# Projection tiles of the prologue as matmul pairs over two column halves of the array

## The chip, the cores and the metric

The kernel runs on one core of one Trainium2 chip. The metric is device time in microseconds (us), lower is better. Per core there are TensorE (PE in the profile; its weight loads are listed as PEld), VectorE (DVE), ScalarE (ACT), GpSimd (POOL) and SyncE (SP), which issues nearly all DMAs here. A matmul holds one operand in the array (128 rows by 128 columns, the "weights", brought in by a weight load of its own) and streams the other one past it; its result goes to PSUM, whose 128 partitions correspond to the columns of the array.

## The reference

One encoder layer over 1024 tokens of width 1024, float32 (cut to what matters):

```python
h = jnp.einsum('bsd,de->bse', x, w_in[layer])
q_a, k_a, v_a, z_a, q_b, k_b, v_b, z_b = jnp.split(h, SPLIT_POINTS, axis=-1)
y_a = neighborhood_attention(q_a, k_a, v_a, rel_pos_bias[layer])      # 8 heads of 64
qb, kb = rotary(q_b, positions), rotary(k_b, positions)
y_b = windowed_gqa_with_sink(qb, kb, v_b, sink_logits[layer])         # 8 q heads, 2 kv heads
mixed = jnp.concatenate([y_a * jax.nn.silu(z_a), y_b * jax.nn.silu(z_b)], axis=-1)
y = jnp.einsum('bse,ed->bsd', mixed, w_out[layer])
x = layer_norm(DEEPNORM_ALPHA * x + y, ln_gain[layer], ln_bias[layer])
```

The projection `x @ w_in` without the v columns is 21 tiles of 128 output columns: four each of q, k and z for group A, four each of qb and zb and one kb for group B.

## The kernel before, in words

Float32 accuracy is had from float16 pairs: x and the weights are scaled by powers of two and split into a high and a low part (`x16h`, `x16l`; `h`, `l` of a weight tile), and a product is three matmuls, high x high, high x low and low x high, summed in PSUM.

The kernel has these stages. The first 59 us bring in x, project v (line L486: tokens as weights, 320 columns of v streamed), and find the scales. Then `project(name)` computes one tile of 128 output columns at a time: for each of two halves of the 1024 tokens it takes a PSUM bank (tag "pj", two of them in turn) and runs 8 blocks of 128 along the width, three products each, so 24 matmuls of 128 x 128 weights with 512 streamed columns into one accumulation group; then `evac` hands the bank to ScalarE, VectorE and GpSimd, which turn it into what q, k or z need. `ORDER` lists the tiles; the first `NPRO = 6` of them (zb0, z0, zb1, kb, qb0, z1) run back to back as a prologue between 59 and 122 us. The other 15 are cut into single matmuls and filled in between the steps of the attention (`pump_to`), which runs from 122 to some 350 us: scores (L816, L817), softmax, products with v (L881). The output projection (L1031) and the layer norm end the kernel.

The order of the instructions of each engine is written by hand: `project` is a generator that yields behind each matmul, `run_to(c)` pumps the prologue matmul by matmul, and `events` are called at fixed counts of yielded steps. In the prologue these events and `project` itself put other work on TensorE between the projection's matmuls: `w_scale` (L225), which sums a statistic of a weight tile over all partitions by one matmul of 2 columns (15 the last time), five times; and `v_scale` (L672), one float32 transpose. These use the whole array. `w_split` readies the weight tiles two ahead (high part on ScalarE, L199, low part on GpSimd, L204 and L205), `sum_w` (L702) and `v_part` (L685, L693) are further work of the prologue on ScalarE and VectorE.

Of the kernel before, what the change touches and what calls it, by code (L numbers as in the profile page):

```python
# [20 lines left out]
KT = D // 128  # L21
# [10 lines left out]
NPRO = 6  # L32
# [29 lines left out]
def hybrid_block(ctx, tc, xT, x, wt, wv, wo, bias, sink, gain, lbias, cos, sin, bmask, out):  # L62
    nc = tc.nc
# [10 lines left out]
    def bank(tag):  # L74
        bufs = {"pj": 2, "s": 4, "t": 2}[tag]
        return (ps1 if bufs == 1 else ps2).tile([128, 512], F32, tag=tag, name=f"ps_{tag}", bufs=bufs)
# [98 lines left out]
    def need(*ops):  # L175
        for op in ops:
            if op.step is None:
                need(*op.deps)
                queues[op.eng].remove(op)
                op.emit()  # L180
# [10 lines left out]
    def w_split(m):  # L191
        if m >= NH:
            return

        def hi():
            h = wp.tile([128, 4, 128], F16, tag="wh", name=f"wh{m}", bufs=4)
            l = wp.tile([128, 4, 128], F16, tag="wl", name=f"wl{m}", bufs=4)
            parts[m] = (h, l)
            nc.scalar.activation(h, raws[m], AF.Copy, scale=scale)  # L199

        def lo():
            h, l = parts[m]
            raw = raws.pop(m)
            nc.gpsimd.tensor_scalar(raw, raw, scale, 1.0, op0=ALU.mult, op1=ALU.mult)  # L204
            nc.gpsimd.tensor_sub(l, raw, h)  # L205

        g = min(m // 2, NPRO)
        scale = wsc[:, g:g + 1]

        o = enq("act", hi, load_ops.get(("w", m)), prio=0.5)  # L210
        o = enq("pool", lo, o, prio=0.5)
        w_ops[m] = o
        if m + 5 < NL:
            load_ops["w", m + 5] = enq("sp", lambda: w_load(m + 5), o)
# [3 lines left out]
    def w_scan(m):  # L218
        nc.scalar.activation(junk[:, :512], raws[m].rearrange("p k c -> p (k c)"), AF.Abs, accum_out=wm[:, m:m + 1])

    def w_scale(n):
        g, v = wg[:, n:n + 1], inv[:, n:n + 1]
        c, m = (2 * n, 2) if n < NPRO else (2 * NPRO, NS)
        ps = bank("t")
        nc.tensor.matmul(ps[:, :m], ones, wm.bitcast(BF16)[:, 2 * c + 1:2 * (c + m):2], start=True, stop=True)  # L225
        nc.vector.tensor_reduce(g, ps[:, :m], axis=mybir.AxisListType.X, op=ALU.add if n < NPRO else ALU.max)
        nc.vector.tensor_scalar_max(g, g, 2.0 ** -30)
        nc.vector.tensor_scalar(g.bitcast(I32), g.bitcast(I32), 0x7F800000, None, op0=ALU.bitwise_and)
        nc.vector.tensor_scalar(wsc[:, n:n + 1].bitcast(I32), g.bitcast(I32), 0x7F800000, None, op0=ALU.bitwise_xor)
        nc.vector.tensor_scalar(v, g, xrs, 0.5, op0=ALU.mult, op1=ALU.mult)  # L230
        nk, nq = ORDER.index("kb"), ORDER.index("qb0")
        if n >= NPRO - 1:
            i = n - NPRO + 1
            nc.vector.tensor_scalar_mul(invt[:, i:i + 1], v, 0.5)
        if n == NPRO:
            for i, (a, b) in enumerate(((nk, nq), (nk, NPRO), (NPRO, NPRO))):
                nc.vector.tensor_scalar(sg[:, i:i + 1], inv[:, a:a + 1], inv[:, b:b + 1], -0.125 / QSCALE ** 2,
                                        op0=ALU.mult, op1=ALU.mult)
            nc.vector.reciprocal(rsg, sg[:, 2:3])
            nc.vector.tensor_reduce(zi[:, 0:1], inv, axis=mybir.AxisListType.X, op=ALU.max)  # L240
            nc.vector.reciprocal(zi[:, 1:2], zi[:, 0:1])
            nc.vector.tensor_scalar_mul(zc[:, 0:1], zi[:, 1:2], MSCALE)
            for i, a in ((1, NPRO - 1), (2, NPRO)):
                nc.vector.tensor_scalar(zc[:, i:i + 1], inv[:, a:a + 1], zi[:, 1:2], 0.5 * MSCALE, op0=ALU.mult, op1=ALU.mult)
            nc.vector.tensor_scalar(mc, zi[:, 0:1], vsc, 0.5 / MSCALE, op0=ALU.mult, op1=ALU.mult)
# [72 lines left out]
    def evac(name, half, ps):  # L318
        sl = slice(512 * half, 512 * half + 512)
        kind = name.rstrip("0123")  # L320
        p = int(name[-1]) if name[-1].isdigit() else 0
        n = ORDER.index(name)
        if kind in ("kb", "qb"):
            raw, o1, o5 = rope(ps, half)
            if kind == "kb":
                split_k("b", half, raw, o5)
            else:
                split_q(f"b{p}", half, raw, o5)
            return [o1]
        if kind == "k":  # L330
            return split_k(p, half, ps)
        if kind == "q":
            return split_q(p, half, ps)
        e = 4 + p if kind == "zb" else p
        if half == 0:
            zt[e] = zslot(f"z{e}", ZTAG.get(name, "z"))
        if name in ORDER[:3]:
            nc.scalar.activation(zt[e][:, sl], ps, AF.Silu, scale=inv[:, n:n + 1])
            return []
        half_inv = invt[:, 0:1] if n < NPRO else invt[:, 1:2]  # L340
        o = enq("act", lambda: nc.scalar.activation(zt[e][:, sl], ps, AF.Tanh, scale=half_inv), prio=0)
        o2 = enq("dve", lambda: nc.vector.scalar_tensor_tensor(
            zt[e][:, sl], zt[e][:, sl], 1.0, ps, op0=ALU.add, op1=ALU.mult), o, prio=0)
        stk_ops.setdefault(name, []).append(o2)
        return [o2]
# [7 lines left out]
    def new_group():  # L353
        if len(groups) >= 2:
            need(*groups[-2])
        return bank("pj")

    def project(name):
        n = ORDER.index(name)
        w_split(2 * n + 2)  # L360
        for half in range(2):
            ps = new_group()
            for k in range(KT):
                if k % 4 == 0:
                    need(w_ops[2 * n + k // 4])
                h, l = parts[2 * n + k // 4]
                if n + 2 < NPRO and half == 0 and k == 4:
                    w_scan(2 * n + 4)
                if n + 2 < NPRO and half == 1 and k == 0:
                    w_scan(2 * n + 5)  # L370
                if half == 0 and k == 4:
                    w_split(2 * n + 3)
                if n + 2 < NPRO and half == 1 and k == 6:
                    w_scale(n + 2)
                for i, (a, b) in enumerate(((h, x16h), (h, x16l), (l, x16h))):
                    mv = b[half, k]
                    if name[0] == "q" and name[1] != "b":
                        mv = mv.rearrange("p (r b c) -> p b r c", b=4, r=8)
                    nc.tensor.matmul(ps, a[:, k % 4, :], mv,  # L379
                                     start=(k == 0 and i == 0), stop=(k == KT - 1 and i == 2))  # L380
                    if not (k == KT - 1 and i == 2):
                        yield
            groups.append(evac(name, half, ps))
            yield
# [20 lines left out]
    with ExitStack() as vctx:  # L405
# [4 lines left out]
        ps = bank("t")  # L410
# [235 lines left out]
        for a in range(2):  # L646
            ps = bank(tags[4 + a])
# [67 lines left out]
        for i in range(NS):  # L715
            at(14 + 14 * i, sum_w, i)
        at(219, w_scale, NPRO)
        fill.extend(project(n) for n in ORDER[:NPRO])
        run_to(100)

# [191 lines left out]
    for b in range(4):  # L912
        at(WIN_AT[b], window, b)
    run_to(48 * NPRO)
    fill.extend(project(n) for n in FILL)
    FILL_N = [48] * len(FILL) + [9, 9, 6, 12, 24]
    pumped = [0]
# [407 lines left out]
```

## Time and profile before

| | us |
|---|---|
| median of 3 runs | 445.9 (445.83 to 446.32) |
| profiled execution, span from its first to its last instruction | 444.7 |
| TensorE busy | 437.5 (98%) |
| VectorE busy | 344.2 (77%) |
| ScalarE busy | 308.3 (69%) |
| GpSimd busy | 221.6 (50%) |

The page gives the profiled execution's own time as its span; the median of the runs stands 1.2 us above it. Busy time of TensorE counts a matmul from its start to its modelled end, and successive matmuls overlap, so a busy share does not tell how fast they follow one another; that is read from the starts in the timeline, or from the chain, which gives the length of a piece and its number of matmuls. "PEclk" is the granted clock of TensorE in tenths of full speed.

### The profile page before, as it was taken

How to read it: one execution, taken by the hardware profiler on the slowest of the kernel's cores; microseconds unless marked ns; L12 is line 12 of the kernel's file. 1: busy time of each engine (PE TensorE's matmuls, PEld its weight loads, DVE VectorE, ACT ScalarE, POOL GpSimd, SP SyncE). 2: the span in 40 equal slices, each digit the busy share in tenths (PEclk: the TensorE clock that was granted, in tenths of full speed). 3: DMA queues.
4: the chain of work that ended last, by engine and by line, in shares of the span. 5: the costliest groups of instructions: out<-in, count | busy, mean ns of one | idle time of the engine just before them, and what ended most of it. 6: DMA issues, size and time to landing. Idle time of an engine off the chain costs nothing.

```text
span 444.7 us, 9505 instructions
## 1 busy us (share of the span) xinstructions
PE 437.5 (98%) x3289; PEld 255.5 (57%) x3289; DVE 344.2 (77%) x849; ACT 308.3 (69%) x700; POOL 221.6 (50%) x235
## 2 busy tenths in 40 slices
PE   9999999999999999999999999999999999999994
PEld 8997754444445565655565655656555654444453
DVE  5978967438986898887988888888878837589944
ACT  5759789766499988887868887888778946302401
POOL 0110074646839558866506767765574405205740
PEclk9999999999999999999999999999999999999997
DMA  8921469984659999587978899998999998103612
GB/s 272 390 91 60 145 235 339 336 292 169 213 127 214 206 190 181 98 162 143 164 127 175 169 182 180 213 170 213 192 204 253 167 172 347 55 0 102 232 69 72
DMA packets 133841, 81.39 MB, mean 183 GB/s; under 512 B 101280, under 2 KB 113440, under 8 KB 133536
## 3 DMA queue, kind: packets, MB, share of 16 engines
q1 hardware_dynamic: 133648, 80.64, 75.4%
q8 instruction: 26, 0.43, 0.4%
q14 instruction: 23, 0.19, 0.2%
q10 hardware_dynamic: 144, 0.13, 0.1%
HBM read 50.34 MB, written 9.96 MB: 136 GB/s over the span
## 4 chain that ended last, share of the span: by engine, by line
PE 91%; DMA 3%; POOL 3%; DVE 1%; issue 1%; ACT 1%; SPq 0%; POOLq 0%; DVEq 0%; ACTq 0%
PE ps_pj L379 44%; PE ps_s L1031 9%; PE ps_s L486 6%; PE ps_t L881 6%; PE ps_pj L1031 5%; PE ps_t L1031 5%; PE ps_s L816 4%; PE ps_s L817 4%; PE ps_pj L486 3%; PE ps_t L486 3%; DMA bias<-in_bias 3%; PE ps_t L901 1%; POOL wl L205 1%; PE ps_t L412 1%; POOL ks L295 1%
## 5 line engine op out<-in xcount | busy, mean ns | idle before, releaser
L379 PE MATMUL ps_pj<-xf,wh 128*128 128x512 f16 x672 | 202.1, 379 | 0.1
L379 PE MATMUL ps_pj<-xf,wl 128*128 128x512 f16 x336 | 127.3, 379 | 0.0
L379 PEld LDWEIGHTS <-wh 128*128 128x128 f16 x672 | 63.7, 98 | 60.4 <-DVE ks L263 0.5
L842 ACT ACTIVATE ps_s<-sn,nm 128x385 f32<-128x385 f32 (+3 forms) x128 | 70.1, 548 | 25.1 <-DVE nm L826 24.6
L853 DVE SCALAR_TENSOR_TENSOR split<-ps_s,split 128x384 f16<-128x384 f32 (+2 forms) x128 | 65.7, 513 | 27.5 <-ACT split L852 25.9
L1031 PEld LDWEIGHTS <-m 128*128 128x128 f16 x432 | 40.0, 98 | 41.1 <-DVE m L939 0.2
L852 ACT ACTIVATE split<-ps_s 128x384 f16<-128x384 f32 (+2 forms) x128 | 57.8, 452 | 2.5 <-DMA tr<-split 0.2
L204 POOL TENSOR_SCALAR wr<-wr,wsc 128x512 f32<-128x512 f32 x26 | 20.6, 791 | 68.1 <-ACT wh L199 61.6
L379 PEld LDWEIGHTS <-wl 128*128 128x128 f16 x336 | 32.9, 98 | 37.4
L826 DVE CUSTOM_DVE_ANT_0 sn<-ps_s,bm,nsk 128x384 f32<-128x384 f32 (+1 forms) x64 | 40.7, 636 | 2.0 <-PE ps_s L817 1.7
L1031 PE MATMUL ps_s<-wo,m 128*128 128x512 f16 (+1 forms) x192 | 40.8, 366 | 0.0
L816 PE MATMUL ps_s<-ks,qs 128*128 128x384 f16 (+4 forms) x128 | 39.2, 306 | 0.3 <-DVE qs L263 0.3
L817 PE MATMUL ps_s<-ks,qs 128*128 128x384 f16 (+4 forms) x128 | 39.2, 306 | 0.0
L826 DVE CUSTOM_DVE_ANT_0 sn<-ps_s,bias,sg 128x264 f32<-128x264 f32 (+1 forms) x64 | 35.0, 547 | 4.5 <-issue 1.5
L881 PEld LDWEIGHTS <-tr 128*128 128x128 f16 (+1 forms) x1104 | 36.6, 98 | 2.2
L205 POOL TENSOR_TENSOR wl<-wr,wh 128x512 f16<-128x512 f32 x26 | 32.7, 1257 | 2.2
L788 POOL TENSOR_SCALAR bias<-bias,rsg 128x552 f32<-128x552 f32 (+1 forms) x24 | 19.1, 797 | 23.8 <-DMA bias<-in_bias 22.6
L295 POOL COPY ks<-ks 64x512 f16<-64x512 f16 x40 | 26.0, 661 | 7.1 <-DVE ks L263 2.8
L1086 ACT ACTIVATE sd<-mv,eps 128x1 f32<-128x1 f32 x8 | 2.4, 295 | 36.5 <-DVE mv L1084 35.2
L1031 PE MATMUL ps_pj<-wo,m 128*128 128x512 f16 (+1 forms) x144 | 26.2, 326 | 0.0
L1130 POOL TENSOR_TENSOR xr<-xr,gb 128x512 f32<-128x512 f32 x7 | 9.8, 1396 | 32.4 <-ACT xr L1127 32.4
L842 ACT ACTIVATION_READ_ACCUMULATOR ps_s<-sn,nm 128x1 f32 x128 | 24.4, 190 | 0.0
(188 smaller groups left out, 813.8 us busy)
## 6 DMA issues: line engine op xcount, KB each, us to landing
ws<-in_wt SPq DMA_DIRECT2D x15, 512.0 KB, 5.9
wr<-in_wt SPq DMA_DIRECT2D x26, 256.0 KB, 3.6
wor<-in_wo SPq DMA_DIRECT2D x22, 256.0 KB, 3.5
bias<-in_bias SPq DMA_DIRECT2D x16, 276.0 KB, 3.3
xr<-in_x SPq DMA_DIRECT2D x8, 512.0 KB, 9.6
out<-xr SPq DMA_DIRECT2D x15, 256.0 KB, 2.1
bias<-in_bias SPq DMA_DIRECT2D x8, 368.0 KB, 3.8
wvraw<-in_wv SPq DMA_DIRECT2D x9, 320.0 KB, 5.8
```

Source lines behind the costliest of these rows:

```text
L205: nc.gpsimd.tensor_sub(l, raw, h)
L295: nc.gpsimd.tensor_copy(t[o, sl], t[a, sl])
L379: nc.tensor.matmul(ps, a[:, k % 4, :], mv, start=(k == 0 and i == 0), stop=(k == KT - 1 and i == 2))
L486: nc.tensor.matmul(ps[:, :320], lh[:, ts], rh[:, cs], start=(k == ko[0] and i == 0), stop=(k == ko[-1] and i == 2))
L816: nc.tensor.matmul(ps[:, :m], q, sl[0], start=True, stop=False)
L817: nc.tensor.matmul(ps[:, :m], q, sl[1], start=False, stop=True)
L826: nc.vector.tensor_tensor_reduce(sn[:, :m], ps[:, :m], bias_t, sg[:, c:c + 1], init, op0=ALU.add, op1=ALU.min, accum_out=nm)
L842: nc.scalar.activation(pt[:, :m], sn[:, :m], AF.Exp, bias=nm, scale=-1.0, accum_out=sm[:, k:k + 1])
L852: nc.scalar.activation(hl[:, :m, 0, :c], src, AF.Copy, scale=PSCALE)
L853: nc.vector.scalar_tensor_tensor(hl[:, :m, 1, :c], src, PSCALE, hl[:, :m, 0, :c], op0=ALU.mult, op1=ALU.subtract)
L881: nc.tensor.matmul(ps[:, HD * m:HD * m + HD], a, b_, start=(i == 0), stop=(i == len(mms) - 1))
L1031: nc.tensor.matmul(ps, lh[:, ts], rh[:, cs], start=(e == EO[0] and i == 0), stop=(e == EO[-1] and i == 2))
```

## The change

For a tile of the prologue (`n < NPRO`), each of the 288 matmuls over the whole array becomes two: one with the weight columns 0 to 63 into PSUM partitions 0 to 63, one with the weight columns 64 to 127 into partitions 64 to 127. Both stream the same 512 columns of x, and each has a weight load of 64 columns ahead of it. In the program's instructions they occupy a tile of 128 rows by 64 columns of the array, the second at column 64. The tiles filled into the attention stay as they are.

```diff
                     mv = b[half, k]
                     if name[0] == "q" and name[1] != "b":
                         mv = mv.rearrange("p (r b c) -> p b r c", b=4, r=8)
-                    nc.tensor.matmul(ps, a[:, k % 4, :], mv,
-                                     start=(k == 0 and i == 0), stop=(k == KT - 1 and i == 2))
+                    for c in (slice(0, 64), slice(64, 128)) if n < NPRO else (slice(0, 128),):
+                        nc.tensor.matmul(ps[c], a[:, k % 4, c], mv,
+                                         start=(k == 0 and i == 0), stop=(k == KT - 1 and i == 2))
                     if not (k == KT - 1 and i == 2):
                         yield
```

The `yield` stays where it was, behind the pair, so the counts at which events are called are unchanged. The order of the instructions on VectorE, ScalarE, GpSimd and SyncE is the same as before, and on TensorE the pairs stand where the single matmuls stood. The first matmul of the second to fifth tile has a wait on an earlier matmul of TensorE's own.

## The prediction

> **What bounds the kernel now.** I read the page's busy times first, then the chain of waits that ended last in order of time, then the busy times of the stretch in which the prologue's projections run, then the waits of TensorE, and last TensorE's groups by shape and its timeline.
>
> The busy times and the throttle row of the 40 slices say which engine to look at:
>
> ```profile
> span 444.7 us, 9505 instructions
> PE 437.5 (98%) x3289; PEld 255.5 (57%) x3289; DVE 344.2 (77%) x849; ACT 308.3 (69%) x700; POOL 221.6 (50%) x235
> PEclk9999999999999999999999999999999999999997
> PE 91%; DMA 3%; POOL 3%; DVE 1%; issue 1%; ACT 1%; SPq 0%; POOLq 0%; DVEq 0%; ACTq 0%
> ```
>
> TensorE is busy for 98% of the span at nearly full clock and makes up 91% of the chain. A busy TensorE can still be one that is badly fed, so the stretch itself must be read. The chain, in order of time, gives it in pieces (start, length, what):
>
> ```profile
> 53.02 6.52 PE ps_t L486 x48
> 59.54 3.45 PE ps_pj L379 x16
> 62.99 0.11 PE ps_s L672
> 63.10 5.61 PE ps_pj L379 x26
> 68.71 0.00 PE ps_t L225
> 68.72 10.38 PE ps_pj L379 x48
> ...
> 107.02 14.91 PE ps_pj L379 x69
> 121.93 0.11 PE ps_s L816
> ```
>
> The six tiles are the L379 matmuls from 59.5 to 121.9 us: 6 tiles x 2 token halves x 8 k blocks x 3 products = 288. One piece holds 48 of them in 10.38 us, so one costs 216.25 ns of TensorE, and 288 cost 62.3 us. The chain hands them on from one to the next with no wait between; the little matmuls of L225 in between take 0.00 of it and the one of L672 takes 0.11. The stretch as a whole, and the waits of TensorE over the whole kernel:
>
> ```profile
> 59.37:121.77 62.40, 62.40 (x297) 28.44 (x294) 41.21 (x93) 45.25 (x81) 38.40 (x39) 1.00 0.79 259
> PE ps_t L1111 <- ACT dr L1109: 1.8, 1, 1.8
> PE ps_t L412 <- DVE warm L127: 1.0, 1, 1.0
> PE ps_s L816 <- DVE qs L263: 0.3, 1, 0.3
> ```
>
> In the stretch's row the columns are length, then busy time of PE, its weight loads, VectorE, ScalarE and GpSimd, the granted clock (1.00), the DMA share and GB/s. TensorE fills all 62.40 us; the next engine, ScalarE, fills 45.25. In the whole kernel TensorE waits 3.1 us for others, and none of that lies between 59 and 122 us. So what the edit does to the spacing of these matmuls goes to the end of the span one for one: no engine waits ahead of them that could give time back, and what follows is again TensorE's own queue.
>
> **The change, part by part.** Each of the 288 matmuls of 128 array columns becomes two of 64, each with a weight load of its own; both stream the same 512 columns of x. TensorE issues 288 matmuls and 288 weight loads more; no other engine's instruction, order or DMA changes. The accumulation groups of the halves lie on different partitions of the same bank, and the evacuation waits for the second half's last matmul.
>
> *The streams.* First, what a matmul costs. The L486 piece has 48 matmuls of 320 columns in 6.52 us, 135.8 ns each; 216.25 less 135.8 over 192 columns is 0.419 ns a column, so 512 columns take 214.5 ns and the fixed part is 1.7 ns. The time is that of the streamed columns. Half the array's columns make a stream no shorter. If the halves stream one after the other, a pair costs 432.5 ns; if they stream side by side, 216 ns. The trace has no matmul on part of the columns, so the two ends are +62.3 us and, if the fixed part were hidden too, 288 x 1.7 = -0.5 us. I take side by side, +0: the halves share no array column, no PSUM partition and no wait, so nothing in the program orders them. The nearest rows show TensorE holding two matmuls in flight: a record lasts 379 ns where the spacing is 216.
>
> ```profile
> L379 PE MATMUL ps_pj<-xf,wh 128*128 128x512 f16 x672 | 202.1, 379 | 0.1
> L379 PEld LDWEIGHTS <-wh 128*128 128x128 f16 x672 | 63.7, 98 | 60.4 <-DVE ks L263 0.5
> 149.73 1.13 PE L881 MATMUL ps_t<-vb,tr 128*128 128x64 f16 x33
> ```
>
> The Trainium skill, page "TensorEngine Tiling (Array Packing)", section "Key Properties", says that different tiles can execute weight loads and matmuls in parallel; no row here shows it.
>
> *Issue and weight loads.* The L881 row has 33 matmuls of 64 columns, each with its own load of 128 columns, in 1.13 us less the last one's drain of 0.16 (379 - 216 ns): some 29 ns for load and matmul together. So TensorE issues two such couples within 60 ns, well under 216. Each load must lie beside the stream of the other half. That loads lie beside streams is what the timeline shows for the whole array:
>
> ```profile
> 62.40 0.38 PE L379 MATMUL ps_pj<-xf,wl 128*128 128x512 f16 x1
> 62.40 0.10 PEld L379 LDWEIGHTS <-wh 128*128 128x128 f16 x1
> 62.61 0.38 PE L379 MATMUL ps_pj<-xf,wh 128*128 128x512 f16 x1
> ```
>
> The load of the next weights begins with the matmul before it (62.40) and lasts 98 ns. Two in a row are 196 ns, still under 216. I take 0, with 98 ns a pair as the other end if that cover is gone (28.2 us, the second rival).
>
> The Trainium skill, page "TensorE: Matmul & The Clock Gate", section "The mechanism", speaks against the change: weight loads overlap matmuls in flight only when the row group differs, and both halves here use all rows. The timeline above differs from that for the whole array, where a load with the same rows overlaps at 62.40; for halves no row decides. By that rule the loads would lie open, and the time would be that of the second rival or above.
>
> *Turning between whole and half array.* Matmuls on the whole array stand inside the stretch: the scale sums of L225 five times and the transpose of L672 once. With the way in from L486 and out to L816 this makes 14 changes of shape. Now they are nearly free:
>
> ```profile
> 78.72 0.38 PE L379 MATMUL ps_pj<-xf,wl 128*128 128x512 f16 x1
> 78.93 0.17 PE L225 MATMUL ps_t<-wm,ones 128*128 128x2 bf16 x1
> 78.96 0.38 PE L379 MATMUL ps_pj<-xf,wh 128*128 128x512 f16 x1
> ```
>
> The sum costs 0.03 us. No row shows a change of shape. At the low end it costs 0 (below it nothing can be gained, as there is only 0.03 to save). At the high end the array empties and the next weights load in the open: 379 - 216 + 98 = 261 ns, in all 3.7 us. I take the array emptying alone, 163 ns, since a different partition of the array cannot take in a stream while the old one's wave still runs, while loads ran beside a matmul in the rows above: 14 x 0.163 = 2.3 us.
>
> The Trainium skill, page "TensorEngine Tiling (Array Packing)", section "Key Properties", says that a change of tiling mode drains TensorE; no row here shows it.
>
> *Waits.* At the first matmul of tiles two to five stands a new wait of TensorE on its own earlier matmul, that of the group before the last in the same bank. That lies a half tile back (48 matmuls, 10.38 us by the chain), so it is long over. Price 0; were it met late, everything after it on TensorE would stand, which is in the range by the rivals.
>
> **Sum.** 444.7 + 0 + 0 + 2.3 = 447.0 us of span. The median of the runs is 445.9, 1.2 above this span for what lies around it, so the forecast is 448.2 us, 0.5% slower; by the ends of the changes of shape 445.9 to 449.6, less 0.5 for hidden fixed parts: 445.4. About 0.2%, 0.9 us, is what a measurement of this kernel can tell from no change.
>
> **The rivals.**
> 1. *Side by side, and the change of shape is free.* If TensorE keeps the waves of old and new shape apart without emptying, nothing is added and the hidden fixed part can give up to 0.5 us back: 445.4 to 446.8. For it: the change from f32 to f16 and back around L672 costs only 0.11. Against: that is no change of shape. It decides from a price below 0.9/14 = 64 ns a change. This one ends on the other side: not slower, and faster beyond 0.9 us only if the halves also spare something that I cannot see.
> 2. *Weight loads in the open.* If a half's load cannot run while that half, or the other, streams, each pair shows one load: 98 ns x 288 = 28.2 us, 476.4 us with the changes of shape; with 29 ns, the spacing of L881, 8.4 us and 456.6. For it: each half has its load directly ahead of its matmul, twice as many as before. Against: the timeline's loads beside streams.
> 3. *No concurrency: the halves take turns.* 62.3 us more, 508.2, and 510.5 with the changes of shape. For it: the trace never shows two streams at one time, only a stream beside a drain. Against: nothing orders them in the program. It would be the case in which the change does not do what splitting columns is able to do.
>
> **How the numbers follow.** Forecast (side by side, array empties) 0.42; rival 1 0.21, of which 0.06 faster and 0.15 within the 0.2%; rival 2 0.18; rival 3 0.19. So faster 0.06, same 0.15, slower 0.79. Rival 3 alone may be left out of the range, the others are in: 445.2 to 477. The likeliest case's own range is 447 to 449.6.
>
> **What would show it.** In the profile of the changed kernel the pairs at the new line have records of 64 x 512; side by side means that the two of a pair start some 30 to 100 ns apart and pairs start 216 ns apart, so that 48 pairs again take about 10.4 us and the first L816 matmul starts near 124 us, not 121.8. The gaps around L225 and L672 give the change of shape: the next matmul behind an L225 some 0.3 us after it is due, not 0.03. Pairs that start 310 ns apart with a load between them speak for rival 2, starts every 216 ns with alternating halves for rival 3, and L816 at 184 us. From 124 us on the kernel should be the old one, shifted; if the rest of the span is longer or shorter by more than 1 us, then the claim that all of it passes on one for one is wrong.

## The result and the profile after

| | us |
|---|---|
| before, median of 11 runs | 446.07 (445.36 to 447.05) |
| changed, median of 11 runs | 447.6 (446.7 to 448.81) |
| ratio changed / before | 1.0031, 95% interval 1.002 to 1.0043 |
| forecast | 448.2, range 445.2 to 477 |

The change makes the kernel slower by 0.3%, 1.4 us by the ratio (0.9 to 1.9). The profiled execution of the changed kernel has a span of 445.7 us, that of before 444.7. In the changed kernel's line numbers L380 is the projection (L379 before), L673 the transpose (L672), L817 the first score matmul (L816). The page of the changed kernel:

```profile
span 445.7 us, 10081 instructions
PE 438.7 (98%) x3577; PEld 259.0 (58%) x3577; DVE 344.4 (77%) x849; ACT 308.4 (69%) x700; POOL 222.0 (50%) x235
```

TensorE has 288 matmuls and 288 loads more, as the edit says; its busy time is 1.2 us longer, the other engines' is the same within 0.4 us. The chain of the changed kernel, in order of time (start, length, what), has the same pieces as before, so each can be laid beside its own:

```profile
58.75 3.58 PE ps_pj L380 x32
62.32 0.25 PE ps_s L673
62.58 5.73 PE ps_pj L380 x52
68.31 0.11 PE ps_t L225
68.42 10.48 PE ps_pj L380 x96
78.90 0.11 PE ps_t L225
79.01 10.48 PE ps_pj L380 x96
...
107.55 15.01 PE ps_pj L380 x138
122.56 0.22 PE ps_s L817
```

A piece of 96 half matmuls takes 10.48 us where 48 whole ones took 10.38. So the halves stream side by side: a pair costs what a whole matmul did. The 0.10 us is paid once in a piece of 48 pairs, not once for each pair, and each L225 costs 0.11 where it cost 0.00, the L673 0.25 where it cost 0.11. From the first projection piece to the first score matmul it is 122.56 - 58.75 = 63.81 us after, 121.93 - 59.54 = 62.39 before: 1.42 us more. That holds 13 of the 14 changes of shape: a piece is counted from the end of the record before it (58.75 is the end of the last L487), so the way in is inside, but the way out stands in the score matmul's own piece, 0.22 where it was 0.11. All 14 together are 1.42 + 0.11 = 1.53 us, 0.109 each. The rest of the span's difference lies outside: the projections began 0.69 us earlier in this execution (58.68 against 59.37 us; in the experiments below between 58.8 and 59.75), and what follows the first score matmul took 0.22 us more.

How two halves lie in the timeline, and what a change of shape looks like (columns: start, duration, engine, line, what; x2 and x4 are merged neighbours):

```profile
67.71 0.38 PE L380 MATMUL ps_pj<-xf,wh 128*64 128x512 f16 x2
67.92 0.38 PE L380 MATMUL ps_pj<-xf,wl 128*64 128x512 f16 x2
68.24 0.10 PEld L225 LDWEIGHTS <-ones 128*128 128x128 bf16 x1 [0.41 <-issue]
68.24 0.18 PE L225 MATMUL ps_t<-wm,ones 128*128 128x2 bf16 x1
68.34 0.14 PEld L380 LDWEIGHTS <-wh 128*64 128x64 f16 x4
68.35 0.62 PE L380 MATMUL ps_pj<-xf,wh 128*64 128x512 f16 x4
68.59 0.11 PEld L380 LDWEIGHTS <-wl 128*64 128x64 f16 x2
```

Two matmuls together span 0.38 us, the record of one: in the trace the second half starts 3 ns behind the first (records start to start, finer than the view prints). Pairs follow at 0.21 to 0.22. The whole-array L225 was due at 67.92 + 0.216 = 68.14 and starts at 68.24, 0.10 late, and its load starts with it, not a stream ahead as in the kernel before. The pair behind it starts 0.11 later, where it took 0.03 before, and the pair after that comes 0.24 behind it (68.59 - 68.35), not 0.216. That is 0.20 us for in and out.

### The profile page after: what moved, and what is told of

Same layout as the page of the kernel before. It is cut to its first block, busy times and chain, and to the rows that moved or that the text cites. A ratio compares the mean times of both kernels' runs of the same rounds, so it can differ in the third digit from the quotient of the medians.

```text
span 445.7 us, 10081 instructions
## 1 busy us (share of the span) xinstructions
PE 438.7 (98%) x3577; PEld 259.0 (58%) x3577; DVE 344.4 (77%) x849; ACT 308.4 (69%) x700; POOL 222.0 (50%) x235
## 4 chain that ended last, share of the span: by engine, by line
PE 94%; DMA 3%; DVE 1%; ACT 1%; issue 1%; POOL 0%; SPq 0%; DVEq 0%; ACTq 0%; POOLq 0%
PE ps_pj L380 46%; PE ps_s L1032 9%; PE ps_t L882 7%; PE ps_s L487 6%; PE ps_pj L1032 5%; PE ps_t L1032 5%; PE ps_s L817 4%; PE ps_s L818 4%; PE ps_pj L487 3%; PE ps_t L487 3%; DMA tr<-split 2%; PE ps_t L902 1%; DMA bias<-in_bias 1%; PE ps_t L413 1%; PE ps_t L1113 0%
## 5 line engine op out<-in xcount | busy, mean ns | idle before, releaser
L380 PE MATMUL ps_pj<-xf,wh 128*128 128x512 f16 (+1 forms) x864 | 202.7, 379 | 0.1
L380 PE MATMUL ps_pj<-xf,wl 128*128 128x512 f16 (+1 forms) x432 | 127.6, 379 | 0.0
L380 PEld LDWEIGHTS <-wh 128*128 128x128 f16 (+1 forms) x864 | 66.5, 103 | 57.3 <-DVE ks L263 0.5
L380 PEld LDWEIGHTS <-wl 128*128 128x128 f16 (+1 forms) x432 | 34.4, 103 | 35.9
L817 PE MATMUL ps_s<-ks,qs 128*128 128x384 f16 (+4 forms) x128 | 39.2, 307 | 0.3 <-DVE qs L263 0.3
```

The source lines that it names most:

```text
L380: nc.tensor.matmul(ps[c], a[:, k % 4, c], mv, start=(k == 0 and i == 0), stop=(k == KT - 1 and i == 2))
L817: nc.tensor.matmul(ps[:, :m], q, sl[0], start=True, stop=False)
```

## The experiments

Two theories were put against each other first. Theory 1: pairs are free, each change of the array's shape costs about 0.10 us (1.42 over 14; with the way out, 1.53 over 14, it is 0.11). Theory 2: each pair costs 5 ns (1.42 over 288). After that come the three rivals of the prediction: what the halves need to run side by side, and how near the weight loads are to lying open. "The stretch" is the time from the first projection matmul to the first score matmul: 62.40 us before, 63.81 in the changed kernel. The halved sums were run 12 times and the quarters 4 times; each of the others is one run, read from the stretch in its profile.

**The scale sums in halves too.** Edit against the changed kernel, in `w_scale`:

```diff
-        nc.tensor.matmul(ps[:, :m], ones, wm..., start=True, stop=True)
+        for h in (slice(0, 64), slice(64, 128)) if n >= 2 else (slice(0, 128),):
+            nc.tensor.matmul(ps[h, :m], ones[:, h], wm..., start=True, stop=True)
```

> The five scale sums of L225 inside the stretch also run as pairs over the two column halves, so that 4 changes of shape are left of 14 (in from the v projection, around the one transpose, out to the scores). Theory 1 (the cost sits in the changes of shape, about 0.10 us each, the chain's 1.42 us over 14): the stretch falls by 10 x 0.10 = 1.0 us against the change, and the time is 0.4 us above before (ratio 1.000 to 1.002). Theory 2 (the cost sits in the pairs, 1.42 us over 288 = 5 ns each): nothing changes against the change, ratio 1.003.

Measured 447.25 us, ratio to before 1.0022 (1.0007 to 1.0037). The interval does not separate the theories. The chain does:

```profile
63.37 5.73 PE ps_pj L381 x52
69.10 10.39 PE ps_pj L381 x96
79.49 10.39 PE ps_pj L381 x96
...
107.44 14.91 PE ps_pj L381 x138
122.35 0.21 PE ps_s L818
```

The pieces are at 10.39, before's 10.38, and the sums take no time of their own, with the same 96 halves in each. The stretch is 62.81 us, 1.00 less than in the changed kernel, as theory 1 said; theory 2 falls.

**Many changes of shape.** Only the third product runs in halves:

```diff
-                    for c in (slice(0, 64), slice(64, 128)) if n < NPRO else (slice(0, 128),):
+                    for c in (slice(0, 64), slice(64, 128)) if n < NPRO and i == 2 else (slice(0, 128),):
```

> Only the third of the three products of each k block runs as a pair of halves, the other two over the whole array: 96 pairs, and 192 changes of shape more. Theory 1 at 0.10 us a change: 192 x 0.10 = 19 us above before. The drain that was assumed in the prediction, 0.163 us: 31 us above. Theory 2 (5 ns a pair): 0.5 us above.

Measured 468.84 us, 22.4 above before's 446.48. The chain (48 products, 16 of them pairs, in a piece), then the timeline:

```profile
71.94 13.90 PE ps_pj L380 x64
85.96 13.91 PE ps_pj L380 x64
```

```profile
79.89 0.38 PE L380 MATMUL ps_pj<-xf,wh 128*128 128x512 f16 x1
80.20 0.41 PE L380 MATMUL ps_pj<-xf,wl 128*64 128x512 f16 x2
80.54 0.60 PE L380 MATMUL ps_pj<-xf,wh 128*128 128x512 f16 x2
81.07 0.41 PE L380 MATMUL ps_pj<-xf,wl 128*64 128x512 f16 x2
```

From one piece to the next it is 85.96 - 71.94 = 14.02 us (the L225 between them, 0.11, holds a change too), and 14.02 - 10.38 = 3.64 us over 32 changes is 0.114 us each. The expectation of the next run was written with 0.110, from 13.90 alone. Starts that should be 0.216 apart are 0.31 into the halves (79.89 to 80.20) and 0.34 out of them (80.20 to 80.54). The stretch is 84.18 us, 21.8 above before. This is theory 1 some fourteen times enlarged (192 changes against 14), and below the 0.163 of the prediction.

**Halves against quarters.** Two products as halves, the third as four quarters of 32 columns; the whole array has no part in these changes:

```diff
+   for c in [slice(32 * r, 32 * r + 32) for r in range(4)] if n < NPRO and i == 2 else (slice(0, 64), slice(64, 128)) if n < NPRO ...
```

> Two products of each k block as pairs of halves, the third as four quarters of 32 columns: 192 changes between two part shapes, none of them with the whole array, beside the 14 of the change. If every change of the array's shape costs the 0.110 us that whole to half and back cost: 192 x 0.110 = 21 us above the change, 468.5. If only the turn between the whole array and parts costs: as the change, 447.5.

Measured 471.56 us, before 446.1 beside it; the stretch is 85.62 us, 21.8 above the changed kernel where 21 was expected; the rest of what the run lost lies behind the stretch (see the quarters below). The chain's pieces of 48 products:

```profile
72.66 14.12 PE ps_pj L380 x128
86.88 14.12 PE ps_pj L380 x128
```

14.12 - 10.48 = 3.64 us over 32 changes, 0.114 each. It is the change of shape itself that costs, not the turn from whole to part.

**Quarters alone.** All products as four quarters:

> Each matmul of the prologue's tiles as four over quarters of 32 columns, in place of two halves. Theory 1 (only changes of shape cost; loads and issue of four lie under one stream of 216 ns): as the change, ratio 1.003. Theory 2 (a cost for each further part, 5 ns): 3 x 5 ns x 288 = 4.3 us above before. If the four weight loads of about 100 ns cannot all lie under a stream: 4 x 98 = 392 ns a group, 50 us above.

Measured 448.85 us, ratio 1.0058 (1.004 to 1.0076). The chain:

```profile
69.26 10.47 PE ps_pj L380 x192
79.84 10.47 PE ps_pj L380 x192
```

Four parts side by side cost what two do (10.47 against 10.48), and the stretch is 63.77 us: theory 1 holds there, theory 2 would have given 10.38 + 0.72. But the whole kernel lost 1.2 us more than the changed one by the ratios, though the two intervals touch (1.004 to 1.0076 here, 1.002 to 1.0043 there). In the one profile that lies behind the first score matmul: 324.6 us from there to the end, 322.9 before. Over the eleven profiles here, all with the same code behind the stretch, that rest lies between 322.3 and 324.6 us. Laid beside before, matmul by matmul, the lag comes in steps at different places in each profile, and the runs of 24 have the same 324.6; why it varies is not settled.

**Neighbours in the same half.** Three products of the first half, then three of the second (here and in the runs below the code is cut to the order of the loops; the tiles of the attention stay as they are):

```diff
-   for i, (a, b) in enumerate(prods):
-       for c in cols:
+   for c in cols:
+       for i, (a, b) in enumerate(prods):
```

> The same half matmuls in another order: per k block three products of the first half, then three of the second, so that neighbours mostly share their half. If two streams run side by side only in different halves, and TensorE starts matmuls in order, a block of six takes four stream lengths of 216 ns, not three: 48 blocks of 16 (96 blocks) x 216 ns = 20.8 us above the change. If TensorE could take halves one after the other at twice the rate, or sort them by itself: no change against the pairs. If it ran them strictly in turn and something else made the pairs cheap: 62 us above.

(The blocks are 96.) Measured 447.46 us in one run, stretch 64.27. The chain:

```profile
69.23 10.49 PE ps_pj L381 x96
79.83 10.49 PE ps_pj L381 x96
```

```profile
80.86 0.39 PE L381 MATMUL ps_pj<-xf,wl 128*64 128x512 f16 x2
81.08 0.60 PE L381 MATMUL ps_pj<-xf,wh 128*64 128x512 f16 x4
81.51 0.39 PE L381 MATMUL ps_pj<-xf,wl 128*64 128x512 f16 x2
```

No change at all, where 20.8 us were expected. Either half matmuls are simply twice as fast, or TensorE starts a matmul of the free half ahead of queued ones of the busy half. In the trace the matmuls start in twos as before, but 10 ns apart (0.39 us for two), where the changed kernel has 3: the partner stands three places later in the program, behind two that start 216 and 432 ns later. The next run was made for this.

**Runs of 24.** All 24 products of the first half, then the 24 of the second:

```diff
-   for k in range(KT):
-       for i, (a, b) in enumerate(prods):
-           for c in cols:
+   for c in cols:
+       for k in range(KT):
+           for i, (a, b) in enumerate(prods):
```

> The halves in runs of 24: all of the first half's products over the 8 k blocks, then all of the second's. In runs of three each the halves overlapped fully, so TensorE starts a matmul of the free half ahead of queued ones of the busy half. With a look-ahead of W matmuls, a group of 48 takes the larger of 24 and 48 - 2W stream lengths: no change for W of 12 or more, 62.3 x (24 - 2W) / 24 above the change for less (W = 8: 21 us; W = 2: 52 us). If the overlap in runs of three came from something else and halves are just twice as fast: no change.

Measured 492.07 us, before 446.53 beside it. Chain and timeline:

```profile
76.47 17.50 PE ps_pj L381 x96
94.09 17.50 PE ps_pj L381 x96
```

```profile
85.12 0.60 PE L381 MATMUL ps_pj<-xf,wh 128*64 128x512 f16 x2
85.55 0.38 PE L381 MATMUL ps_pj<-xf,wl 128*64 128x512 f16 x1
85.56 0.81 PE L381 MATMUL ps_pj<-xf,wh 128*64 128x512 f16 x4
86.01 0.56 PE L381 MATMUL ps_pj<-xf,wl 128*64 128x512 f16 x2
86.23 0.60 PE L381 MATMUL ps_pj<-xf,wh 128*64 128x512 f16 x2
```

Within a run, half matmuls follow one another every 216 ns (85.12 to 85.55 for two): half the columns do not make a stream shorter, and in one half they take turns. Where runs meet, at 85.56, pairs appear for a short while, then single ones again: from 85.55 to 86.23 eight matmuls start, the last four of one run and the first four of the next. 17.50 us is 81 streams for 96 matmuls, so 15 lie beside another, 3.75 at each of the four borders. With W = 3.75 the formula gives 42.8 us above the changed kernel; the stretch is 106.78 us, 43.0 above it. (That W is taken from the same run, so this shows only that the whole stretch goes like the one piece.) The overlap needs different halves and reaches some four matmuls ahead in the queue.

**Shorter streams, to lay the loads open.** Edit of the 256 run; 128 likewise, and the comparison with the whole array in place of the two halves:

```diff
-   for c in cols:
-       nc.tensor.matmul(ps[c], a[:, k % 4, c], mv, start=(k == 0 and i == 0), stop=...)
+   for f in range(2):
+       s = slice(256 * f, 256 * f + 256)
+       for c in cols:
+           nc.tensor.matmul(ps[c, s], a[:, k % 4, c], mv[:, s], start=(k == 0 and i == 0 and f == 0), stop=...)
```

> As the change, but each half matmul streams its 512 columns as two of 256, each with a weight load of its own: a pair has 108 ns of stream in place of 216, and still two loads whose records last 110 ns each. If the loads of the two halves go side by side and beside the streams (theory 1): 288 more fixed parts of 1.7 ns, 0.5 us above the change, 448. If the two loads of a pair go one behind the other at the 110 ns of their records: 220 ns a pair of 256, 576 x 112 ns = 64 us above. If one at the 29 ns that load and matmul took in the products with v: hidden, 448.

Measured 448.21 us; stretch 64.54, 0.73 above the changed kernel: 2.5 ns for each of the 288 matmul pairs more, where 1.7 was expected.

> The comparison to the run before: the whole array, as in the kernel before, but streams of 128 columns, 1152 matmuls with 1152 loads in the stretch. 54 ns of stream against 29 ns for load and issue: only the fixed parts come on top, 864 x 1.7 = 1.5 us above before, 448.

Measured 447.42 us; stretch 64.56, 2.2 above before, again 2.5 ns for each of the 864 matmuls more.

> As the change, but streams of 128 columns: 1152 pairs with 54 ns of stream each. If loads of both halves go side by side and beside the streams: 864 fixed parts of 1.7 ns, some 2 us above the change, 449. If a pair's two loads take 2 x 29 = 58 ns in turn: 1152 x (58 - 54) = 5 us above, 452. If a pair shows the 110 ns of a load's record: 1152 x 56 = 64 us above, 512.

Measured 466.0 us; stretch 81.96. The chain of the whole array at 128 columns first, then the timeline of the halves, pieces of their chain, their waits of TensorE and their queue of instruction packets:

```profile
68.43 10.74 PE ps_pj L384 x192
```

```profile
76.10 0.66 PE L384 MATMUL ps_pj<-xf,wh 128*64 128x128 f16 x16
76.55 0.44 PE L384 MATMUL ps_pj<-xf,wl 128*64 128x128 f16 x8
76.77 0.44 PE L384 MATMUL ps_pj<-xf,wh 128*64 128x128 f16 x9
```

```profile
75.24 3.76 PE ps_pj L384 x128
79.00 1.33 issue
```

```profile
89.44 7.34 PE ps_pj L384 x256
125.84 8.96 PE ps_pj L384 x256
```

```profile
PE ps_pj L384 <- issue: 12.2, 10, 2.3
```

```profile
q8 instruction: 41, 0.67, 0.6%
```

The whole array goes at 10.74 / 192 = 55.9 ns. The halves do 24 matmuls, 12 pairs, from 76.10 to 76.77, 56 ns a pair: two loads in each 56 ns, though a load's record lasts 110 ns, and none shows. So the loads never come near to lying open at 216 ns. The 17.4 us between the two runs are something else that no theory had: ten holes of up to 2.3 us in which TensorE waits for nothing the profile shows, 12.2 us together (13.8 if they are counted from start to start of the matmuls around them).

The trace tells what the holes are. The packets of queue q8 hold 16384 bytes each, and their number follows TensorE's matmuls and loads divided by 256: 7154 / 256 = 27.9 with 28 packets in the changed kernel, 10610 / 256 = 41.4 with 41 here. So a packet is 256 instructions of TensorE, 128 matmuls with their loads. All ten holes lie at such a border: between their ends TensorE runs 128 matmuls or a multiple (the x128 and x256 pieces above). And each ends 1.0 to 1.5 us after a packet has landed; for the hole at 79.00 the packet took from 77.65 to 78.86, and TensorE resumed at 80.34. TensorE waits there for its next instructions. With streams of 256 columns a packet lasts twice as long, lands 2.9 us or more before TensorE reaches the border in the stretch, and there is no hole. No run changed the supply itself.

Of the 17.4 us the holes are 13.8 and the changes of shape 1.4. Most of what is left is a stretch behind the hole that ends at 125.84: there the granted clock is 0.51 for 3.4 us and a pair costs 107 ns, so that 256 half matmuls take 8.96 us from 125.84, where the piece at 89.44 took 7.34. What lowers the clock there no run here tells: the holes that end at 75.24 and 103.36 are as long or nearly so, and the clock stays at 1.00 behind them.

## Why the prediction was right, point by point

*The bound.* Right. TensorE's spacing in the stretch went to the end one for one: 1.42 us more in the stretch, 1.4 by the ratio. With 21.8 us more in the stretch, the third-product run took 22.4 us more.

*The streams.* Right: +0. The pieces at 10.39 in the run with halved sums show it to 0.01 us in 48 pairs; runs of 24 show that serial halves would have cost 216 ns each, the price of rival 3. The reason given, that nothing in the program orders the halves, was argued only; the runs show that TensorE treats the halves as separate, even out of program order. By the Trainium skill, page "TensorE: Matmul & The Clock Gate", section "The mechanism", packed tiles start about 4 ns apart; the trace agrees, with 3 ns. The same section of the Trainium skill says that matmuls start strictly in program order; the runs of three and of 24 differ from that, and the measurement decides.

*Weight loads.* Right: 0. Rival 2's condition, loads that cannot lie beside a stream, is refuted for halves with 216, 109 and 56 ns a pair. The rule of the Trainium skill, same page and section, that loads overlap only when the row group differs does not hold here. One size was wrong: the prediction had the two matmuls of a pair start 30 to 100 ns apart, from the 29 ns that a load and a matmul took in L881; they start 3 ns apart. It cost the forecast nothing, as the term stands at 0 either way.

*Changes of shape.* That the changes of shape alone cost was right, the size was not: 14 x 0.163 = 2.3 us was forecast, 1.53 measured, 0.109 a change here and 0.114 in the two runs with 192 more. The term that was too large is the array's emptying at 379 - 216 = 163 ns. In the changed kernel the new shape's load and matmul start 91 to 95 ns after the last stream ends (as its 213 to 216 ns count from its start), and 24 ns more come behind the first pair of halves; behind an L225 the next matmul is 0.21 us late, where the prediction named 0.3 as the sign. Since record ends are modelled, 163 ns was a row for something else than the time in which the array is blocked; that the forecast of 448.2 us came as near as 0.6 us to the measured time is in part luck. Rival 1, with its point at 64 ns a change, is refuted. What these 95 ns consist of, the array's emptying or another thing, stays open: they are 95 to 106 before loads of 32, 64 and 128 columns around L225, which speaks against the load's length.

*Waits.* The new wait of TensorE on its own group cost nothing: the pieces before and behind it are at the price of the others. The distance was misread: a half tile is 24 products, 5.2 us, and 48 in 10.38 us are a whole tile. The wait is long over at 5.2 us too.

*Rest of the span.* The claim that it stays within 1 us held for the change (323.1 against 322.9 us), not for the quarters (324.6), the runs of 24 (324.6) and the halves against quarters (324.4), and that scatter is unexplained. The first score matmul came at 122.5 us and not near 124, as the projections began 0.69 us earlier in this execution and the changes of shape cost less.

## What to carry to other kernels

Splitting full-width matmuls over column parts of the array gains nothing when TensorE is the bound, since a matmul takes the time of the columns it streams, however few columns of the array it uses; it costs about 0.11 us each time the array's shape changes. Four matmuls of 32 columns went in the time of one, so parts can only pay where a matmul leaves columns empty, and then all matmuls of a stretch should have one shape, down to the small ones: halving five small sums took 1.0 of the stretch's 1.42 us away. Matmuls of different parts must stand near one another in the program: runs of three in one part cost nothing, runs of 24 cost 43 us.

## What was not expected of the hardware

- TensorE starts matmuls of a free column half ahead of queued ones of the busy half, some four matmuls deep: runs of three cost nothing, runs of 24 cost 43 us.
- Two loads of 64 columns and two matmuls go through in 56 ns, though each load's record lasts 110 ns.
- At that rate TensorE outran its instructions: with 1152 pairs it stood still ten times for up to 2.3 us, each time at the border of a packet of 256 of them.
- A change of the array's shape costs 0.109 to 0.114 us, less than a matmul's record beyond its stream (0.163 us).
